# Gated delta rule: decay matrices from rows of running sums instead of a matrix product, and another table of stages

## The chip, the cores and the metric

The kernel runs on one core of one Trainium2 chip. The metric is the device time of one execution in microseconds (us), as the median of three runs. Engines: PE multiplies matrices, DVE and ACT work elementwise, POOL (GpSimd) does slower elementwise work, SP only issues DMAs.

## What is computed

Two decoder layers over 2048 tokens of width 1024: a gated delta rule (8 heads of 128), then an attention layer with forget gates. The change lies in the first. Cut to what matters:

```
gcum  = cumsum(g)                                   # g: log decay, per token and head
diff  = gcum[..., :, None] - gcum[..., None, :]
decay = where(causal, exp(diff), 0)
a_mat = where(strict, (beta k) k^T * decay, 0)
sol   = triangular_solve(I + a_mat, [beta v, beta k exp(gcum)])
attn  = q k^T * decay
# then, chunk by chunk: v_new = u - w S;  o = q exp(g) S + attn v_new;  S = S exp(g_last) + k_dec^T v_new
```

In the kernel a chunk has 128 tokens, and `decay` of one head is a tile E of 128x128 for each of the four chunks of a quarter.

## The kernel before, in words

The delta-rule phase takes the first 1185 us or so. It runs over four quarters of 512 tokens, and in each over four pairs of heads. `project` (L272) makes one pair: for each head the tiles k, q, v (in this order, kinds 1, 0, 2; tile number `ct` = kind x 8 + head), then two z tiles. A tile is eight k-steps of three 128x512 matmuls (`mm3`, L129 to L132: float32 split in a high and a low part), collected in a PSUM buffer `pp`, which ACT and DVE empty a little later (`cx`, `acc`, `th`, `kq`; transposes `pt`). In quarter 0 the weights are loaded as they are (`wr`), cast on ACT (`wh`), the rest taken on POOL (`wl`, L296), and both kept in DRAM (`w_d`) for the other quarters.

Ahead of a head's first tile L325 to L332 make its E: POOL multiplies an upper triangle with g, as a high and a low part (`rg`, two instructions), PE multiplies both with a strict lower triangle (`pdf`, L329, two matmuls), which gives all the differences of running sums, ACT takes the exp from PSUM (L331), POOL sets what lies above the diagonal to zero (L332).

`finish` (L418) inverts the unit triangular matrices of a pair and runs the recurrence. Diagonal blocks of 32x32 go to DRAM and back in another layout (`d1`, `Ai`), DVE eliminates (`tmp`, `Ti`), the blocks return (`d2`, `At`), DVE transposes three of four (`Tn`, L447). Small products on PE then join blocks to 64 (`px` L453, copied to `X` by ACT L457 and DVE L458; `py` L464) and to 128 (`px` with 64x64, `py` with 64x64). After that comes the recurrence (`pa`, `o`, `R`, `w`, `S`), then the norm and the gate (`og`).

`weave` (L589) runs the two together: at every k-step of the current pair's `project` the previous pair's `finish` may take a step; a `yield n` in `finish` lets n further k-steps pass. The stage lengths stand in one line (L583): `W_INV` k-steps between the start of the inverse and `px`, `W_PY` from `px` to `py`, and so on. A scheduler of the framework sets the final order of each engine when the kernel is built, going by the order of the program; each engine then runs its own list in order and waits for semaphores. An SP, ACT or POOL instruction that waits therefore holds up all that stands behind it on its engine.

## Time and profile before

| | |
|---|---|
| three runs | 2913.45, 2918.45, 2922.11 us; median 2918.45 |
| the profiled execution | 2933.14 us, its span 2931.4 us |
| mean granted clock of PE | 0.982 of full speed |
| PE busy | 2814.7 us, 96% |
| DVE, ACT, POOL busy | 1718.0 (59%), 1334.9 (46%), 707.4 (24%) us |
| moved by DMA | 371.64 MB |

Durations below come from the profiled execution. In a timeline row the first number is the start in us, the second the busy time of the row's instructions, `x2` their count, and the bracket the idle time of the engine before it and what ended that. Buffer numbers are left out of names, so `pp_q` is any projection tile of that kind.

### The profile page before, as it was taken

Reading aid. Unit: us, or ns where it says so; the run is one execution under the profiler, and the core shown is the slowest. Engines: PE = TensorE matmul, PEld = TensorE weight load, DVE = VectorE, ACT = ScalarE, POOL = GpSimd, SP = SyncE. Lnnn points to the kernel's source line nnn. Section 1 sums busy time; section 2 is a strip of 40 time slices with the busy share of each in tenths; the row PEclk is TensorE's granted clock in tenths of the full one; section 3 lists DMA queues with packets and bytes.
Section 4 is the critical chain, followed back from the end, with each engine's and each line's share of the span. In section 5 each row is a group of like instructions: output and inputs, shape, how many; then the busy total and the mean of one; then the engine's idle time right before and its main releaser. Section 6 shows DMA issues by size and latency. Waiting matters only on the chain. (4 is left out here: it accounts for less than half of the span.)

```text
span 2931.4 us, 50710 instructions
## 1 busy us (share of the span) xinstructions
PE 2814.7 (96%) x18406; PEld 2446.1 (83%) x18406; DVE 1718.0 (59%) x5053; ACT 1334.9 (46%) x3695; POOL 707.4 (24%) x713
## 2 busy tenths in 40 slices
PE   7898999999999999989999999999999999999998
PEld 5677788878887878778999999999997888888787
DVE  5767876777777776644333124332228888888422
ACT  4445544454445444434344223443326777776421
POOL 5544211111111111123211000110004444443322
PEclk9999999999999999989999999999999999999999
DMA  6565544444453443645322233332322332332443
GB/s 222 177 185 187 170 135 138 151 148 150 136 160 120 150 147 107 193 127 181 94 87 87 92 97 112 97 97 93 102 76 87 101 97 91 98 93 81 151 144 108
DMA packets 295505, 371.64 MB, mean 127 GB/s; under 512 B 68443, under 2 KB 216150, under 8 KB 294230
## 3 DMA queue, kind: packets, MB, share of 16 engines
q1 hardware_dynamic: 295254, 368.39, 39.6%
q8 instruction: 145, 2.38, 0.3%
q14 instruction: 106, 0.87, 0.1%
HBM read 263.40 MB, written 104.92 MB: 126 GB/s over the span
## 5 line engine op out<-in xcount | busy, mean ns | idle before, releaser
L130 PE MATMUL pp_q<-xh_q,wh_q 128*128 128x512 f32 x768 | 327.4, 426 | 3.4 <-ACT wh_q L294 1.9
L132 PE MATMUL pp_q<-xh_q,wl_q 128*128 128x512 f32 x768 | 308.8, 402 | 0.0
L131 PE MATMUL pp_q<-xl_q,wh_q 128*128 128x512 f32 x768 | 307.5, 400 | 0.0
L351 DVE SCALAR_TENSOR_TENSOR acc_q<-cx_q,cols,acc_q 128x512 f32<-128x512 f32 x288 | 225.9, 784 | 13.3 <-ACT acc_q L349 10.0
L125 DVE TENSOR_TENSOR pl<-pt,ph 128x512 fp32r<-128x512 f32 (+1 forms) x320 | 191.8, 605 | 39.5 <-ACT ph L124 37.6
L124 ACT CAST ph<-pt 128x512 fp32r<-128x512 f32 (+1 forms) x320 | 161.6, 519 | 92.8 <-PE pt L1077 91.9
L354 ACT ACTIVATE th_q<-acc_q 128x512 f32<-128x512 f32 x96 | 60.6, 632 | 285.7 <-DVE acc_q L351 282.3
L1063 ACT ACTIVATE s<-s,nm 128x128 f32<-128x128 f32 (+15 forms) x128 | 154.2, 1205 | 73.6 <-DVE nm L1061 73.4
L1077 PE MATMUL pt<-ident,s 128*128 128x128 f32 x1088 | 173.8, 274 | 2.7 <-DVE pl L125 2.4
L132 PEld LDWEIGHTS pp_q<-xh_q,wl_q 128*128 128x128 f32 x768 | 146.7, 191 | 34.9 <-POOL wl_q L296 0.4
L130 PEld LDWEIGHTS pp_q<-xh_q,wh_q 128*128 128x128 f32 x768 | 146.9, 191 | 29.8 <-ACT wh_q L294 2.0
L131 PEld LDWEIGHTS pp_q<-xl_q,wh_q 128*128 128x128 f32 x768 | 147.4, 192 | 26.3
L1077 PEld LDWEIGHTS pt<-ident,s 128*128 128x128 f32 x1088 | 134.5, 141 | 33.3 <-DVE pl L125 3.5
L130 PE MATMUL ppk<-wh_k,hh 128*128 128x256 f32 x512 | 148.2, 289 | 2.6 <-issue 2.6
L130 PE MATMUL ppq<-wh_q,hh 128*128 128x256 f32 x512 | 146.8, 287 | 0.0
L131 PE MATMUL ppk<-wl_k,hh 128*128 128x256 f32 x512 | 145.0, 283 | 0.0
L130 PE MATMUL ppv<-wh_v,hh 128*128 128x256 f32 (+1 forms) x512 | 144.9, 283 | 0.0
L132 PE MATMUL ppk<-wh_k,hl 128*128 128x256 f32 x512 | 144.8, 283 | 0.0
L130 PE MATMUL ppz<-wh_z,hh 128*128 128x256 f32 x512 | 144.3, 282 | 0.0
L132 PE MATMUL ppv<-wh_v,hl 128*128 128x256 f32 (+1 forms) x512 | 144.0, 281 | 0.0
L131 PE MATMUL ppv<-wl_v,hh 128*128 128x256 f32 (+1 forms) x512 | 143.9, 281 | 0.0
L132 PE MATMUL ppq<-wh_q,hl 128*128 128x256 f32 x512 | 143.7, 281 | 0.0
(479 smaller groups left out, 8592.7 us busy)
## 6 DMA issues: line engine op xcount, KB each, us to landing
wh_q<-w_d SPq DMA_DIRECT2D x72, 512.0 KB, 3.7
wl_q<-w_d SPq DMA_DIRECT2D x72, 512.0 KB, 5.0
wr_q<-in_gdn_w_in_dram SPq DMA_DIRECT2D x24, 512.0 KB, 6.4
w_d<-wh_q SPq DMA_DIRECT2D x24, 512.0 KB, 4.7
w_d<-wl_q SPq DMA_DIRECT2D x24, 512.0 KB, 3.5
wh_q_z<-w_d SPq DMA_DIRECT2D x24, 512.0 KB, 3.5
wl_q_z<-w_d SPq DMA_DIRECT2D x24, 512.0 KB, 4.4
x_q<-in_x_dram SPq DMA_DIRECT2D x16, 512.0 KB, 4.2
```

The costliest lines, as they stand in the source:

```text
L124: i = k.nc.scalar.copy(hi, src)
L125: (eng or k.nc.vector).tensor_tensor(out=lo, in0=src, in1=f(hi), op=ALU.subtract)
L130: nc.tensor.matmul(out, ah, bh, start=start, stop=False)
L131: nc.tensor.matmul(out, ah, bl, start=False, stop=False)
L132: nc.tensor.matmul(out, al, bh, start=False, stop=stop)
L351: nc.vector.scalar_tensor_tensor(out=acc, in0=cx[:, j:j + TB], scalar=cw[j], in1=acc, op0=ALU.mult, op1=ALU.add)
L354: nc.scalar.activation(th, acc, AF.Tanh, scale=0.5)
L1063: e = nc.scalar.activation(s[:, 0:w], s[:, 0:w], AF.Exp, bias=nm, accum_out=ls[:, ii:ii + 1])
L1077: nc.tensor.transpose(out=pt[:, ii * P:(ii + 1) * P], in_=Ps[ii][:, j * P:(j + 1) * P], identity=k.ident)
```

## The change

The preparation of a quarter no longer splits g. It transposes the running sums `gc` (a PE transpose, 128x32 to 32x128), copies them to SBUF (`gT`) and keeps another copy (`gs`) beside. `decays`, called after a head's q tile, replaces the product: for the first head of a quarter it writes `gT` to DRAM (`g_d`) and loads that head's row, spread over all partitions, into `gb`, both on POOL's DMA queue; for every head but the last it issues the load of the next head's row on SP's queue (256 KB in SBUF). POOL then subtracts the column `gs` from the row, sets what lies above the diagonal to a large negative number, and ACT takes the exp from SBUF into E. In the table, `W_INV` goes from 45 to 43, `W_PY` from 5 to 6, `W_PY2` from 2 to 3; the total is the same.

```diff
-        gh = p2.tile([P, CH, H], F32R, tag="gh", name=f"gh_{q_}")
-        nc.vector.tensor_copy(gh, g)
-        gl = p2.tile([P, CH, H], F32R, tag="gl", name=f"gl_{q_}")
-        nc.vector.tensor_tensor(out=gl, in0=g, in1=f(gh), op=ALU.subtract)
...
+        pgT = pq.tile([CH * H, P], F32, tag="kkq", name=f"pgT_{q_}")
+        nc.tensor.transpose(out=pgT, in_=gcf[:, 0, :], identity=k.ident)
+        gT = p1.tile([CH * H, P], F32, tag="gT", name=f"gT_{q_}")
+        nc.vector.tensor_copy(gT, pgT)
+        g_d = pd.tile([CH, H, P], F32, tag="g_d", name=f"g_d_{q_}")
+        gs = p2.tile([P, CH, H], F32, tag="gs", name=f"gs_{q_}")
+        nc.vector.tensor_copy(gs, gc[:, 0])
...
+        def rows(h, dma):
+            gb = gbs[h] = p2.tile([P, CH, P], F32, tag="gb", name=f"gb_{q_}_{h}")
+            dma.dma_start(gb, g_d[:, h].unsqueeze(0).to_broadcast([P, CH, P]))
+
+        def decays(h, E):
+
+            if h == 0:
+                nc.gpsimd.dma_start(g_d.rearrange("c h t -> (c h) t"), gT)
+                rows(0, nc.gpsimd)
+            if h < H - 1:
+                rows(h + 1, nc.sync)
+            gb = gbs.pop(h)
+            nc.gpsimd.tensor_tensor(out=gb, in0=gb, in1=gs[:, :, h:h + 1].to_broadcast([P, CH, P]), op=ALU.subtract)
+            nc.gpsimd.affine_select(out=gb, in_=gb, pattern=[[0, CH], [1, P]], compare_op=ALU.is_ge,
+                                    fill=NEG, base=0, channel_multiplier=-1)
+            nc.scalar.activation(E, gb, AF.Exp)
...
-            rg = p1.tile([P, 2, CH, P], F32R, tag="rg", name=f"rg_{q_}_{h}")
-            for i, gg in enumerate((gh, gl)):
-                nc.gpsimd.tensor_tensor(out=rg[:, i], in0=bc(k.tri, CH),
-                                        in1=f(gg[:, :, h:h + 1]).to_broadcast([P, CH, P]), op=ALU.mult)
-            pdf = pq.tile([P, CH, P], F32, tag="kkq", name=f"pdf_{q_}_{h}")
-            for i in range(2):
-                nc.tensor.matmul(pdf.rearrange("p a b -> p (a b)"), k.lowr,
-                                 rg[:, i].rearrange("p a b -> p (a b)"), start=i == 0, stop=i == 1)
-            nc.scalar.activation(E, pdf, AF.Exp)
-            nc.gpsimd.affine_select(out=E, in_=E, pattern=[[0, CH], [1, P]], compare_op=ALU.is_ge,
-                                    fill=0.0, base=0, channel_multiplier=-1)
...
+                if kind == 0:
+                    decays(h, E)
...
-W_INV, W_PY, W_PX2, W_PY2, W_A, W_B, W_C, W_OUT, W_OUT2 = 45, 5, 4, 2, 2, 1, 2, 9, 1
+W_INV, W_PY, W_PX2, W_PY2, W_A, W_B, W_C, W_OUT, W_OUT2 = 43, 6, 4, 3, 2, 1, 2, 9, 1
```

How the built order of the engines differs, at two places. The first is the inverse of the first head pair of quarter 1 (`q1g`), while the v tile of head 3 (`pp_q_19`) is projected. A row is line, operation, output and inputs with buffer numbers, size, and what it waits for (`DMAHW`: a transfer). On PE, before:

```order
L130 MATMUL pp_q_19_4810<-xh_q_6_3318,wh_q_19_4806 128x512
L131 MATMUL pp_q_19_4810<-xl_q_6_3326,wh_q_19_4806 128x512
L132 MATMUL pp_q_19_4810<-xh_q_6_3318,wl_q_19_4807 128x512
L366 MATMUL pt_q_11_4844<-ident,kq_q_3_4632 128x128 [waits DVE_49]
L366 MATMUL pt_q_11_4844<-ident,kq_q_3_4632 128x128 x3
L453 MATMUL px_q1g_4861<-Tn,At_q1g_3454 32x32 [waits DVE_49,PE_49]
L453 MATMUL px_q1g_4861<-Tn,At_q1g_3454 32x32 [waits DVE_49]
L453 MATMUL px_q1g_4861<-Tn,At_q1g_3454 32x32 x14
L130 MATMUL pp_q_19_4810<-xh_q_7_3319,wh_q_19_4806 128x512
```

On PE there, after:

```order
L124 MATMUL pp_q_19_4804<-xh_q_4_3308,wh_q_19_4800 128x512
L125 MATMUL pp_q_19_4804<-xl_q_4_3316,wh_q_19_4800 128x512
L126 MATMUL pp_q_19_4804<-xh_q_4_3308,wl_q_19_4801 128x512
L460 MATMUL px_q1g_4832<-Tn,At_q1g_3449 32x32 [waits DVE_49,PE_49]
L460 MATMUL px_q1g_4832<-Tn,At_q1g_3449 32x32 [waits DVE_49]
L460 MATMUL px_q1g_4832<-Tn,At_q1g_3449 32x32 x14
L124 MATMUL pp_q_19_4804<-xh_q_5_3309,wh_q_19_4800 128x512
```

`px` has moved from behind k-step 6 and the transposes `pt` to behind k-step 4.

On DVE at the same place, before:

```order
L359 SCALAR_TENSOR_TENSOR kq_q_3_4632<-th_q_11_4741,acc_q_11_4736 128x4x128 [waits Activation_49]
L558 SCALAR_TENSOR_TENSOR og_q_6_4788<-pto_q_6_4779,hon,zT_q0g_2425 128x512 [waits PE_49]
L447 STREAM_TRANSPOSE Tn<-At_q1g_3454 32x8x32 [waits DMAHW0_49]
L447 STREAM_TRANSPOSE Tn<-At_q1g_3454 32x8x32 [waits DMAHW1_49]
L346 COPY halo<-cx_q_3_4794 128x3 [waits Activation_49]
L447 STREAM_TRANSPOSE Tn<-At_q1g_3454 32x8x32 [waits DMAHW2_49]
L351 SCALAR_TENSOR_TENSOR acc_q_3_4798<-cx_q_3_4794,cols,acc_q_3_4798 128x512 [waits Activation_49]
```

On DVE there, after:

```order
L565 SCALAR_TENSOR_TENSOR og_q_6_4775<-pto_q_6_4766,hon,zT_q0g_2421 128x512 [waits PE_49]
L366 SCALAR_TENSOR_TENSOR kq_q_3_4627<-th_q_11_4728,acc_q_11_4723 128x4x128 [waits Activation_49]
L454 STREAM_TRANSPOSE Tn<-At_q1g_3449 32x8x32 [waits DMAHW4_49]
L353 COPY halo<-cx_q_3_4788 128x3 [waits Activation_49]
L358 SCALAR_TENSOR_TENSOR acc_q_3_4792<-cx_q_3_4788,cols,acc_q_3_4792 128x512 [waits Activation_49]
L454 STREAM_TRANSPOSE Tn<-At_q1g_3449 32x8x32 [waits DMAHW5_49]
L454 STREAM_TRANSPOSE Tn<-At_q1g_3449 32x8x32 [waits DMAHW6_49]
```

The first `acc` of tile 3 has moved ahead of the second and third `Tn`, and `og` ahead of `kq`.

On ACT at the same place, before:

```order
L349 ACTIVATE acc_q_3_4798<-pp_q_3_4748,cols 128x512
L354 ACTIVATE th_q_3_4803<-acc_q_3_4798 128x512 [waits DVE_49]
L370 ACTIVATE j_q_11_0_4849,ssn_q_3_4644<-pt_q_11_4844 128x128 [waits PE_49,Activation_49,Pool_49]
L370 ACTIVATE j_q_11_1_4851,ssn_q_3_4644<-pt_q_11_4844 128x128 [waits Activation_49]
L370 ACTIVATE j_q_11_2_4853,ssn_q_3_4644<-pt_q_11_4844 128x128 [waits Activation_49]
L370 ACTIVATE j_q_11_3_4855,ssn_q_3_4644<-pt_q_11_4844 128x128 [waits Activation_49]
L373 ACTIVATE kd_q_3_4634<-pt_q_11_4844,eg_q_3450 128x128 x4
L457 COPY X_q1g_4878<-px_q1g_4861 32x256 [waits PE_49]
```

On ACT there, after:

```order
L326 ACTIVATE E_q_4_5066<-gb_q_4_4781 128x512 [waits DVE_49,Pool_49]
L361 ACTIVATE th_q_11_4728<-acc_q_11_4723 128x512 [waits DVE_49]
L407 ACTIVATE vR_q_2_4261<-pt_q_18_4757,vs_q_2_4266 128x128 [waits PE_49]
L407 ACTIVATE vR_q_2_4261<-pt_q_18_4757,vs_q_2_4266 128x128 x3
L352 COPY cx_q_3_4788<-pp_q_3_4735 128x512 [waits PE_49]
L356 ACTIVATE acc_q_3_4792<-pp_q_3_4735,cols 128x512
L464 COPY X_q1g_4849<-px_q1g_4832 32x256 [waits PE_49]
L361 ACTIVATE th_q_3_4797<-acc_q_3_4792 128x512 [waits DVE_49]
```

The copy `X` has moved from behind `th`, `j` and `kd` to straight behind `acc`; the exp of a later head's E stands some rows ahead.

The second place is POOL at the first heads of quarter 0, before:

```order
L325 TENSOR_TENSOR rg_q_0_344<-tri,gh_q_321 128x512 [waits DVE_49]
L325 TENSOR_TENSOR rg_q_0_344<-tri,gl_q_323 128x512 [waits DVE_49]
L296 TENSOR_TENSOR wl_q_16_448<-wr_q_16_449,wh_q_16_447 128x256 [waits DMAHW0_49,Activation_49]
L296 TENSOR_TENSOR wl_q_16_448<-wr_q_16_449,wh_q_16_447 128x256 x3
L325 TENSOR_TENSOR rg_q_1_516<-tri,gh_q_321 128x512 [waits PE_49]
L332 AFFINE_SELECT E_q_0_343<-E_q_0_343 128x512 [waits Activation_49]
```

On POOL there, after:

```order
L318 DMA g_d_q_327<-gT_q_325 32x128 [waits DVE_49]
L295 TENSOR_TENSOR wl_q_16_449<-wr_q_16_450,wh_q_16_448 128x256
L313 DMA gb_q_0_427<-g_d_q_327 128x4x128 [waits DMASW0_49]
L295 TENSOR_TENSOR wl_q_9_521<-wr_q_9_522,wh_q_9_520 128x256 [waits DMAHW3_49,Activation_49]
L295 TENSOR_TENSOR wl_q_9_521<-wr_q_9_522,wh_q_9_520 128x256 x3
L323 TENSOR_TENSOR gb_q_0_427<-gb_q_0_427,gs_q_328 128x512 [waits DMASW1_49]
L323 TENSOR_TENSOR gb_q_1_429<-gb_q_1_429,gs_q_328 128x512 [waits DMAHW5_49]
L324 AFFINE_SELECT gb_q_0_427<-gb_q_0_427 128x512 [waits Pool_49]
```

E of head 0 now hangs on two transfers one after the other and on what stands between them on POOL; the exp of that E stands on ACT ahead of `cx` and `acc` of tile 0.

## Rows read from the trace of the kernel before

**Rows 1.** The page, part 1: busy us, share and instructions of each engine.

```profile
PE 2814.7 (96%) x18406; PEld 2446.1 (83%) x18406; DVE 1718.0 (59%) x5053; ACT 1334.9 (46%) x3695; POOL 707.4 (24%) x713
```

**Rows 2.** Waits of PE, 0 to 1260 us: releaser, us in total, times, longest.

```profile
PE py_q1g L464 <- ACT X_q1g L457: 3.3, 4, 1.1
...
PE pdf_q L329 <- POOL rg_q L325: 2.0, 5, 0.7
...
PE py_q2g L464 <- ACT X_q2g L457: 1.9, 2, 0.9
...
PE py_q1g L464 <- DVE X_q1g L458: 0.9, 4, 0.2
```

**Rows 3.** Timeline of PE, 475 to 477 us, one decay product.

```profile
475.84 0.71 PE L329 MATMUL pdf_q<-rg_q,lowr 128*128 128x512 f32 x2
476.38 0.40 PE L130 MATMUL pp_q<-xh_q,wh_q 128*128 128x512 f32 x1
...
477.09 0.39 PE L130 MATMUL pp_q<-xh_q,wh_q 128*128 128x512 f32 x1
```

**Rows 4.** Timeline of PE, 452 to 460 us, `px` and `py` of `q1g`.

```profile
452.70 0.24 PE L453 MATMUL px_q1g<-Tn,At_q1g 32*32 32x32 f32 x2
453.35 0.69 PE L453 MATMUL px_q1g<-Tn,At_q1g 32*32 32x32 f32 x30 [0.40 <-DVE Tn L447]
...
459.35 0.24 PE L464 MATMUL py_q1g<-At_q1g,X_q1g 32*32 32x32 f32 x2 [0.93 <-ACT X_q1g L457]
```

**Rows 5.** Timeline of DVE, 450 to 455 us.

```profile
450.46 0.69 DVE L359 SCALAR_TENSOR_TENSOR kq_q<-th_q,acc_q 128x512 f32<-128x512 f32 x1 [0.49 <-ACT th_q L354]
...
451.74 0.89 DVE L447 STREAM_TRANSPOSE Tn<-At_q1g 32x256 f32<-32x256 f32 x2
...
452.86 0.43 DVE L447 STREAM_TRANSPOSE Tn<-At_q1g 32x256 f32<-32x256 f32 x1
453.32 1.54 DVE L351 SCALAR_TENSOR_TENSOR acc_q<-cx_q,cols,acc_q 128x512 f32<-128x512 f32 x2
```

**Rows 6.** Timeline of ACT, 451 to 459 us.

```profile
451.80 0.73 ACT L349 ACTIVATE acc_q<-pp_q,cols 128x512 f32<-128x512 f32 x1
...
458.94 0.36 ACT L457 COPY X_q1g<-px_q1g 32x256 f32<-32x256 f32 x1
```

**Rows 7.** Timeline of PE at 590 us, `px` in the v tile of head 7.

```profile
590.70 0.69 PE L453 MATMUL px_q1g<-Tn,At_q1g 32*32 32x32 f32 x32
```

**Rows 8.** Timeline of DVE there.

```profile
589.41 0.44 DVE L447 STREAM_TRANSPOSE Tn<-At_q1g 32x256 f32<-32x256 f32 x1
```

**Rows 9.** Timeline of ACT at 48 us, tile 0 of quarter 0.

```profile
48.44 0.70 ACT L349 ACTIVATE acc_q<-pp_q,cols 128x512 f32<-128x512 f32 x1
```

**Rows 10.** Timeline of PE at 54 us, the first matmul of tile 9.

```profile
54.29 0.39 PE L130 MATMUL pp_q<-xh_q,wh_q 128*128 128x512 f32 x1
```

**Rows 11.** Timeline of PE at 201 and at 304 us, two waits.

```profile
201.21 0.66 PE L366 MATMUL pt_q<-ident,kq_q 128*128 128x128 f32 x4 [1.72 <-DVE kq_q L359]
...
304.32 0.85 PE L453 MATMUL px_q0g<-Tn,At_q0g 32*32 32x32 f32 x30 [2.25 <-DVE Tn L447]
```

**Rows 12.** The page, part 6: DMA issues, KB each, median us to landing.

```profile
wl_q<-w_d SPq DMA_DIRECT2D x72, 512.0 KB, 5.0
```

**Rows 13.** The tile `d_q1g`: issue to landing of its transfers.

```profile
DMA to landing us min/median/max: 1.5/2.0/3.9
```

**Rows 14.** Stretches: length, busy and (count) of PE, PEld, DVE, ACT, POOL, PE clock, DMA share, GB/s.

```profile
201.00:208.00 7.00, 6.79 (x40) 5.90 (x41) 7.00 (x15) 2.81 (x13) 4.54 (x5) 1.00 0.72 206
226.20:233.00 6.80, 4.49 (x40) 3.64 (x41) 4.98 (x11) 4.59 (x17) 4.08 (x4) 0.50 0.46 178
304.70:308.10 3.40, 3.40 (x25) 2.76 (x20) 1.78 (x4) 2.99 (x14) 0.00 (x0) 0.50 0.43 128
461.70:465.10 3.40, 3.40 (x11) 2.75 (x10) 2.91 (x7) 1.66 (x9) 0.26 (x1) 0.50 0.04 10
```

**Rows 15.** Timeline of POOL, 438 to 447 us.

```profile
443.38 1.64 POOL L119 TENSOR_TENSOR rn_q<-ssn_q,mhalf 128x8 f32<-128x8 f32 x1 [2.13 <-DVE ssn_q L376]
```

More of the change, by code (lines that the diff above doesn't have):

```diff
@@ L58, in setup @@
     sb0 = sp.enter_context(k.tc.tile_pool(name="sb0", bufs=1, side="left"))
-    low = sb0.tile([P, P], F32, name="low")
-    nc.gpsimd.affine_select(out=low, in_=k.ones, pattern=[[-1, P]], compare_op=ALU.is_gt,
-                            fill=0.0, base=0, channel_multiplier=1)
-    k.lowr = cp.tile([P, P], F32R, name="lowr")
-    nc.vector.tensor_copy(k.lowr, low)
     k.mhalf = cp.tile([P, 8], F32, name="mhalf")
@@ L191, in gdn @@
     kept = []
+    gbs = {}
     def keep():
@@ L268, in prep @@
         nc.vector.tensor_scalar(out=neg, in0=eg[:, 0], scalar1=-1.0, scalar2=None, op0=ALU.mult)
-        return xh, xl, beta, gh, gl, eg, neg
+        return xh, xl, beta, gs, (gT, g_d), eg, neg
     def project(qt, hg, state, tiles):
-        xh, xl, beta, gh, gl, eg, neg = state
+        xh, xl, beta, gs, (gT, g_d), eg, neg = state
         q_ = f"q{qt}"
```

## The prediction

> **What bounds the kernel now.** I read the busy line of the page first: PE is busy 2814.7 us of a 2931.4 us span [rows 1]. Where PE is that full, a saving counts only if it takes an instruction out of PE's stream or shortens a stretch in which PE stands still. So next came PE's list of waits for the part that the change touches [rows 2], and then PE, DVE and ACT row by row around one inverse, that of the first head pair of quarter 1, at 450 to 460 us [rows 4 to 6]. The reader is to see there a race that is lost by a hair: PE comes to the small products `px`, starts the first two at 452.70, and finds the last transposed tile `Tn` 0.40 us late [rows 4]. Of the twelve head pairs of quarters 1 to 3, six look like that (`px` lies in the v tile of head 3 or head 5; I call them A). Three have `px` in the v tile of head 7 (C): there the last `Tn` ended 0.85 us before `px` began, 589.41 + 0.44 against 590.70 [rows 7, 8]. The last three (D) fall into the next quarter and have more room still.
>
> **What goes: the decay products.** Each of 32 heads loses two 128x512 matmuls `pdf` on PE. The pair starts at 475.84 and the next projection matmul at 476.38, and three projection matmuls behind it take 477.09 - 476.38 = 0.71, that is 0.237 each [rows 3]. So a pair is worth 0.47 (two such steps) to 0.54 (start to start); I take the first, since it is the pitch of everything around it: 32 x 0.466 = **-14.9 us**, and -17.3 at the other end. All of it lies on PE, hence on the path. PE also waited 2.0 us, five times, for POOL's factor `rg` [rows 2]; nobody on PE waits for the new `gb` directly: **-2.0**. The POOL products, the exp on ACT and the mask on POOL are replaced one for one or fall away on engines that PE does not wait for there; they count as nothing, and the cover is gone only where a head's E comes late (below).
>
> **What is added on PE.** Four transposes of the running sums, one a quarter, at about a projection step each (0.24) [rows 3]: **+1.0**. The other additions of the preparation (two small copies on DVE) stand between `gc` and the exp of `eg`, and PE has projection steps to do there.
>
> **What is moved: the W table.** The total of steps is the same; the first stage is two steps shorter, the second and the fourth one longer. As the order shows, `px` stands two k-steps (six matmuls) and four transposes earlier in the v tile: 6 x 0.237 + about 0.5 = 1.9 us less of PE's time in front of it. PE therefore stands at `px` at 452.70 - 1.9 = 450.8. What does DVE do meanwhile? In before it runs without a break from 450.46: `kq`, `og`, two `Tn`, the third `Tn` at 452.86 to 453.3, then the first `acc` of the next tile at 453.32 [rows 5]. In after the `og` comes ahead of `kq` and fills the 0.49 that DVE idled for ACT, so the first `Tn` ends some 0.5 earlier than 452.2, at 451.75; but the second and third stand behind the `acc` of tile 3, and that needs ACT's `acc`, which ends at 451.80 + 0.73 = 452.53 [rows 6]. A DVE `acc` takes 0.77 (1.54 for two) and a `Tn` 0.44 [rows 5]: 452.53 + 0.77 + 0.88 = 454.2. So PE waits 1.0 at the first product and then until 454.2, 3.2 in all against 0.40: +2.8, six times: **+16.8**. For C the order puts one `Tn` behind one `acc`: 589.41 + 0.77 + 0.44 = 590.6 against PE's arrival at 590.70 - 1.9 = 588.8, **+1.7 each, 5.1**. In D there is room: 0.
>
> The other end of these waits. Ahead of that stretch DVE stands for POOL's `rn`, 1.64 us long, and POOL loses one of its three operations of a head. If DVE got that time back, the waits of A would shrink to about 1.6 and those of C to nearly nothing; but POOL had itself been idle for 2.13 us until DVE's `ssn` came, so there is no queue to shorten [rows 15]. If ACT's `acc` is held up by the exp of E, which in after stands a few rows ahead of it, they grow by at most its length, about that of an `acc`, 0.73. I take the plain reading of the rows.
>
> **What it pays back: `py`.** In before the copy of `X` on ACT stood behind eight small activations and began at 458.94, 5 us after `px` was done, and PE waited 0.93 for it at 459.35 [rows 4, 6]. In after the copy stands straight behind `px` on ACT, and `py` has one step more. So these waits go: 3.3 + 1.9 + 1.9 on ACT's half (quarter 3's line reads like quarter 2's) and 2.5 on DVE's (three lines of 0.9, 0.9 and 0.7, the first of them in the rows) [rows 2]: **-9.6**. To bring them back ACT would have to be some 5 us late.
>
> **Quarter 0's first head.** Its row is the one load that nothing precedes: g to DRAM and back on POOL's queue. No POOL-queue transfer is in the trace; the nearest landings are loads of 512 KB on SP's queue at 5.0 us, and the small ones of the inverse at 2.0 us [rows 12, 13]. Two of 2 to 5 us from about 38 us on give 43 to 48; POOL then has four weight pieces, the subtraction and the mask to do, so E's exp would end at 51 to 53, and behind it on ACT stand `cx` and `acc` of tile 0, whose `acc` ran at 48.44 in before; PE needs that PSUM buffer at 54.29, less the two `pdf` pairs ahead of it now gone, 53.4 [rows 9, 10]. The wait is 0 to 5; I take **+2**. SP's queue holds the second head's row ahead of two weight transfers and its third head's row, which waits for the exp of the first E, ahead of a weight load; what that delays is read and split well ahead of its use, and I leave it inside those 0 to 5. In quarters 1 to 3 the first product with E comes a k, a q and half a v tile after the sums are there, so the same chain is covered. The rows themselves (32 loads of 256 KB) go by DMA engines that PE does not wait for: nothing.
>
> The Trainium skill speaks against the POOL-queue DMAs: "SBUF — State Buffer", section "SBUF: two separate sides", says that descriptors of a DMA issued on GpSimd wait while VectorE runs a two-port operation, and gives about 620 ns alone against 3100 ns beside one. No run here shows it. By that figure the two first loads would be some 5 us later in all, an estimate, and the sum 5 us higher; the sum here goes by the bounds above.
>
> **The clock.** A wait of 1.72 us at 201.21 was followed by the full granted clock (1.00, that is 2.4 GHz, from 201 to 208), one of 2.25 at 304.32 by 3.4 us at half of it (0.50, 1.2 GHz), and the waits around 226 us by 6.8 us of half clock [rows 11, 14]. At half clock 3.4 us do the work of 1.7. The waits that I expect in A come as 1.0 and 2.2, between the first two rows: I charge half of 6 x 1.7: **+5.1** (0 to 10.2). The half clock after two of the `py` waits (461.7 to 465.1 is one of the two [rows 14]) goes: **-3.4**.
>
> **The sum:** -14.9 - 2.0 + 1.0 + 16.8 + 5.1 - 9.6 + 2.0 + 5.1 - 3.4 = **+0.1 us**. The profiled execution took 2933.14 us against a median of 2918.45; the sum is a difference within that one execution, and I carry it to the median: 2918.5. Ends of the terms give -18 to +20 around it.
>
> **Rivals.** (1) *The `px` waits don't grow.* DVE comes to `Tn` two to three us earlier against PE, because it has to run a backlog off there (from 450.46 to 454.8 it has no gap) that began some tiles before, where its order has changed too: E comes from SBUF early, and nothing waits for a mask. For it: with `py` without waits each pair's inverse goes on sooner; against it: the `acc` that stands between the `Tn` and hangs on ACT, and a POOL without a queue [rows 5, 15]. It leaves out 16.8, 5.1 and 5.1: -27 + 0.1, **2892**, faster. (2) *The clock falls at every `px`.* The place is the v tile of nine head pairs; the point from which it decides is a wait of about 2.25 us, where rows show half clock. Price: two windows (6.8 us, 3.4 lost) after each of six, one after each of three: 20.4 + 5.1 instead of 5.1, that is +20: **2939**, slower. For it: 1.0 + 2.2 is above the mark as a whole; against it: a product runs between the pieces. (3) *The table does not do what it says*, the first stage is short enough already and the order hardly alters `px`: the order shows otherwise, so no chance of its own.
>
> **How the numbers follow.** The forecast has a chance of 0.48, its own range 2903 to 2932; rival 1 has 0.25, rival 2 0.27. A measurement of this kernel can tell about 0.3% from no change, that is 2909.7 to 2927.2. The forecast puts 0.13 below that, 0.28 within and 0.07 above; rival 1 0.25 below; rival 2 0.02 within and 0.25 above. So faster 0.38, same 0.30, slower 0.32. The range that leaves out two in ten reaches to both rivals: 2890 to 2941.
>
> **What would show it.** The `pdf` rows gone and POOL's `rg` with them; the `px` rows of A with about 3 us of waiting, of C with 1.7, `py` with none; PE's busy time less by about 15 us before clock; the first `acc` of tile 0 near 52 us. The forecast is wrong if the `px` waits stay under 1 us (rival 1), or if the granted clock reads 0.5 after each of them (rival 2); also if a projection waits for weights whose loads stand behind a row load on SP.

## The result and the profile after

The changed kernel takes 2949.65 us against 2918.77 us of the kernel before on the same chip: ratio 1.0102, 95% interval 1.0088 to 1.0116, about 30 us slower. The forecast was no change (2918.5), the range ended at 2941. 2949.65 is the median of four executions, of which one took 3354.11 us at a mean granted clock of 0.761; without that one, which the ratio leaves out, it is 2949.1. The profiled execution of after took 2946.1 us, its span 2944.3.

The page of after, part 1 (busy us, share, instructions), answers to [rows 1]:

```profile
PE 2803.7 (95%) x18346; PEld 2442.4 (83%) x18346; DVE 1698.6 (58%) x5052; ACT 1336.2 (45%) x3695; POOL 678.6 (23%) x688
```

PE has 60 instructions less (64 `pdf` gone, 4 transposes new), and is busy 11 us less than in [rows 1]. So the product is gone, and yet the kernel is slower: the time went into standing still and into clock. PE's waits, 28 to 1290 us (releaser, us in total, times, longest), answer to [rows 2]:

```profile
PE px_q0g L460 <- DVE Tn L454: 15.2, 5, 4.9
PE pt_q L373 <- DVE kq_q L366: 13.1, 6, 5.1
PE pp_q L124 <- ACT acc_q L356: 6.5, 4, 2.6
PE px_q2g L460 <- DVE Tn L454: 6.0, 3, 2.3
PE px_q1g L460 <- DVE Tn L454: 6.0, 3, 2.3
PE px_q3g L460 <- DVE Tn L454: 6.0, 3, 2.3
PE pa_q0g L506 <- DVE vR_q L541: 5.8, 4, 2.7
PE pp_q L124 <- DVE zT_q0g L421: 5.5, 1, 5.5
```

The waits at `rg` have left the list, and those at `py` are down to 0.6 us in all, as forecast. In their place stand nine waits at `px` (three a quarter in quarters 1 to 3, 6.0 us each quarter) and waits of the projection and of `pa`, of which only one, 2.56 us for the first `acc`, was forecast. PE, then DVE and ACT at the first pair of quarter 1, timelines, answer to [rows 4, 5]:

```profile
460.70 0.24 PE L460 MATMUL px_q1g<-Tn,At_q1g 32*32 32x32 f32 x2
463.20 0.69 PE L460 MATMUL px_q1g<-Tn,At_q1g 32*32 32x32 f32 x30 [2.26 <-DVE Tn L454]
464.88 0.63 PE L124 MATMUL pp_q<-xh_q,wh_q 128*128 128x512 f32 x1
465.31 0.63 PE L125 MATMUL pp_q<-xl_q,wh_q 128*128 128x512 f32 x1
```

```profile
460.04 0.43 DVE L454 STREAM_TRANSPOSE Tn<-At_q1g 32x256 f32<-32x256 f32 x1
461.47 0.75 DVE L358 SCALAR_TENSOR_TENSOR acc_q<-cx_q,cols,acc_q 128x512 f32<-128x512 f32 x1 [0.42 <-ACT acc_q L356]
462.25 0.90 DVE L454 STREAM_TRANSPOSE Tn<-At_q1g 32x256 f32<-32x256 f32 x2
```

```profile
460.70 0.73 ACT L356 ACTIVATE acc_q<-pp_q,cols 128x512 f32<-128x512 f32 x1
```

This is the mechanism of the forecast: the second and third `Tn` stand behind an `acc` that waits for ACT (the last row, of ACT, answers to [rows 6]). But look at the matmuls behind it: they start 0.43 apart instead of 0.237. The clock has fallen. Stretches (length, busy and count of PE, PEld, DVE, ACT, POOL, then PE's granted clock, DMA share, GB/s):

```profile
457.40:460.80 3.40, 3.40 (x19) 2.56 (x17) 3.00 (x6) 2.09 (x7) 0.00 (x0) 1.00 0.12 43
464.30:467.70 3.40, 3.40 (x12) 2.70 (x11) 2.29 (x5) 0.99 (x4) 0.00 (x0) 0.50 0.46 128
467.70:471.10 3.40, 3.40 (x29) 2.51 (x31) 0.66 (x2) 2.88 (x13) 0.00 (x0) 1.00 0.91 53
600.80:604.20 3.40, 3.40 (x36) 2.71 (x33) 3.15 (x6) 0.99 (x2) 0.00 (x0) 0.51 0.90 321
365.30:372.10 6.80, 4.69 (x18) 4.20 (x19) 6.16 (x21) 3.01 (x10) 2.39 (x2) 0.50 0.53 162
```

Full clock (1.00, 2.4 GHz) before the wait at 460.94, 3.4 us at half (0.50, 1.2 GHz) behind it, then full again. The fourth row is a pair C, where the wait was 1.46 us; the fifth the first head of quarter 1. Of the nine pairs A and C, eight have such a stretch; a wait of 2.24 us at 1039 has none.

What a whole pair costs is seen in stretches from one pair's first `px` to the next's. Before (a second profiled execution, 2922.12 us, span 2920.4), then after:

```profile
518.60:586.70 68.10, 66.52 (x437) 54.98 (x437) 49.04 (x172) 30.74 (x105) 8.65 (x7) 1.00 0.47 151
667.30:735.00 67.70, 66.36 (x437) 54.92 (x436) 48.93 (x168) 31.25 (x107) 10.65 (x9) 1.00 0.44 137
```

```profile
460.80:529.80 69.00, 66.74 (x433) 55.28 (x433) 47.02 (x168) 30.89 (x107) 8.79 (x7) 0.98 0.51 151
685.20:750.20 65.00, 65.00 (x434) 54.05 (x434) 47.13 (x167) 30.79 (x107) 8.98 (x7) 1.00 0.51 159
```

The last row is a pair without wait: PE busy from end to end, 65.0 us. The same pair of before is the row at 667.30. That is what the rows are worth: 2.7 us there, half of it work (66.36 to 65.0) and half idle time. The row above it, at 460.80, is a pair with a `px` wait: 69.00 - 66.74 = 2.26 of idle time, and about the *same* work now takes 66.74 instead of 65.0, 1.7 more, which is half of 3.4 us. Together 4.0, and the pair is slower than before (68.1).

Added up over the trace of both, in us (I sum PE's idle time, count half of PE's busy time at half clock as lost, and call the remainder work; the second execution of before is the base):

| stretch | before | after | work | idle | half clock |
|---|---|---|---|---|---|
| to `px` of the 4th pair | 382.7 | 391.2 | -9.0 | +12.6 | +4.9 |
| nine intervals inside quarters | 611.2 | 614.7 | -13.9 | +4.1 | +13.2 |
| three intervals over a quarter's turn | 248.7 | 262.5 | -3.7 | +7.0 | +10.3 |
| the rest of the program | 1677.8 | 1675.9 | -0.2 | +1.2 | -2.8 |
| span | 2920.4 | 2944.3 | -27.0 | +25.0 | +25.9 |

The split is rough: kernels with more waits show less work, so idle time and clock are charged somewhat too high and work too low by as much. The sums are exact: everything is lost before the 16th pair, nothing in the attention layer.

One execution can be a chance, but span and mean granted clock are on record for every run, and span x (1 - clock) is what the clock took. It took 37.5 us on average in the 64 executions of before that ran beside the experiments, and 73.7 in the other three of after; what is left of the span is 2880.8 and 2873.0. At full clock after would thus be some 8 us faster than before; the clock costs it 36 us more. Up to 6 of these are half clock during waits, where it costs nothing (24.3 us at half clock against 12.8 in the two profiled executions, at half weight).

### The profile page after: what moved, and what is told of

Read it like the earlier page. It is cut to its first block, busy times and chain, and to the rows that moved or that the text cites. A ratio compares the mean times of both kernels' runs of the same rounds, so it can differ in the third digit from the quotient of the medians.

```text
span 2944.3 us, 50701 instructions
## 1 busy us (share of the span) xinstructions
PE 2803.7 (95%) x18346; PEld 2442.4 (83%) x18346; DVE 1698.6 (58%) x5052; ACT 1336.2 (45%) x3695; POOL 678.6 (23%) x688
## 4 chain that ended last, share of the span: by engine, by line
PE 64%; DVE 15%; issue 5%; ACT 3%; DMA 3%; POOL 2%; SPq 0%; DVEq 0%; POOLq 0%; ACTq 0%
DVE acc_q L358 4%; PE pt L1084 4%; PE ps L126 2%; PE ppv L124 2%; PE ppq L124 2%; PE pp_q_z L124 2%; PE ppv L125 2%; PE ppv L126 2%; PE ppq L125 2%; PE ppq L126 2%; PE ppwf L126 2%; PE ppwf L125 2%; PE ppwf L124 2%; PE ppk L124 2%; PE ps L124 2%
## 5 line engine op out<-in xcount | busy, mean ns | idle before, releaser
L124 PE MATMUL pp_q<-xh_q,wh_q 128*128 128x512 f32 x768 | 336.9, 439 | 13.8 <-ACT acc_q L356 6.5
L125 PE MATMUL pp_q<-xl_q,wh_q 128*128 128x512 f32 x768 | 314.1, 409 | 0.0
L124 PEld LDWEIGHTS pp_q<-xh_q,wh_q 128*128 128x128 f32 x768 | 150.5, 196 | 41.3 <-ACT acc_q L356 8.2
L125 PE MATMUL ppq<-wl_q,hh 128*128 128x256 f32 x512 | 143.7, 281 | 0.0
```

The lines of the kernel that those rows point to most:

```text
L124: nc.tensor.matmul(out, ah, bh, start=start, stop=False)
L125: nc.tensor.matmul(out, ah, bl, start=False, stop=False)
```

## The experiments

Theories as the expectations name them: A, two prices, that of the table (`px` waits and clock) and that of the first heads; B, the table alone; C, the row transfers as such; D, the exp of E waits for a free E buffer; E, ACT loses because it stands in order at that exp. (The pairs A, C and D of the prediction have nothing to do with these letters.) Each ratio is to the kernel before on the same chip. A "due step" in the expectations is a k-step.

### Table and rows apart

`e1_rows_old_table` is after with `45, 5, 4, 2` in the table; `e2_product_new_table` is before with the new one:

```diff
-W_INV, W_PY, W_PX2, W_PY2, ... = 45, 5, 4, 2, ...
+W_INV, W_PY, W_PX2, W_PY2, ... = 43, 6, 4, 3, ...
```

> The changed kernel with the table of before (45, 5, 4, 2): rows from DRAM alone. Theory A (the added 31 us are two prices, the table's waits at px with half clock behind them, and the first head of each quarter that waits for its row; the product's 15 us on PE are saved): the table's price goes, the first heads' stays, and the waits at py of 0.9 us come back: 2920 to 2935 us, with waits of PE at px below 1.6 us in quarters 1 to 3 and the waits of the first projection after E at 364 us unchanged (about 1.4 and 2.7 us). Theory B (the table alone): 2900 to 2908. Theory C (the rows alone, by their transfers): 2945 to 2955.

> The kernel before with the new table (43, 6, 4, 3): the stages alone. Theory A: the waits at px of about 2.3 us in the v tiles of heads 3 and 5 and about 1.5 us in that of head 7, each followed by 3.4 us of half clock, and no waits at py: 2928 to 2940 us. Theory B (the table alone): 2955 to 2965 us, since the product's matmuls are still there. Theory C (the rows alone): 2913 to 2923 us.

Measured: e1 2935.35 us, 1.0064 (1.0039 to 1.0089); e2 2935.27, 1.0056 (1.0037 to 1.0075). Each half costs about 16 us, and the two add up. Theories B and C fall by both runs as the whole cause, and so does the thought that either half was good; theory A has e2 and misses e1 by 0.35 us. In e2 there is no row load at all; `px` waits there 1.36 + 0.83:

```profile
454.85 0.21 PE L453 MATMUL px_q1g<-Tn,At_q1g 32*32 32x32 f32 x2 [1.36 <-DVE Tn L447]
455.89 0.69 PE L453 MATMUL px_q1g<-Tn,At_q1g 32*32 32x32 f32 x30 [0.83 <-DVE Tn L447]
```

In the nine intervals inside quarters e2 has 14.3 us of idle time against 12.3 before: what `px` costs, `py` had cost before, so in idle time the table is nearly free. But its half-clock stretches there come to 34 us, against none, and the nine take 625.9 against 611.2. That execution is the slowest of e2's seven (2943.0 us). Over all seven the clock took 50.3 us against 37.5 in before, and 2883.0 is left against 2880.8: the table's price is clock. The rows alone (e1) leave 2872.0, 9 less than before, and the clock takes 60.9.

A second look at before itself belongs here:

> The kernel before, unchanged, for a second profile on this chip: its first profiled execution took 2933 us and its timed ones 2913 to 2922. All theories: 2912 to 2935 us; which stretches differ between its two profiles shows how much of a stretch's difference to the changed kernel is the kernel.

It took 2922.12 us, where the first profiled execution had taken 2933.14. The half clock at 461.7 [rows 14] isn't there in the second one, nor behind any other `py` wait of 0.93 inside quarters 1 to 3. The same code at the same places had half clock in one execution and not in the other.

### The first head of a quarter

`e6_first_head_product` is after with the product for head 0 of each quarter, and rows for heads 1 to 7 (`gT` to DRAM on SP):

```diff
+            if h == 0:
...
+                    nc.tensor.matmul(pdf.rearrange("p a b -> p (a b)"), k.lowr,
+                                     rg[i].rearrange("p a b -> p (a b)"), start=i == 0, stop=i == 1)
+                nc.scalar.activation(E, pdf, AF.Exp)
```

> The changed kernel, but the first head of each quarter takes its E from the matrix product as before, so no E waits for the trip to DRAM and back; the running sums are written to DRAM on SP's queue, the other seven heads load rows as in the change. Eight matmuls of 0.23 us come back. Theory A: PE's waits of 2.6 us at 54 us, and of 1.4 and 2.7 us at 364 and 1.9 and 2.6 at 660 us go with the half clock behind them: 2925 to 2937 us. Theory B (the table alone) and C by the transfers as such: 2945 to 2953 us, since 28 of 32 rows are still loaded and the table is the new one.

Measured: 2940.3 us, 1.0083 (1.0061 to 1.0106): 9 less than after by the medians, but the intervals of the two ratios overlap, and it lies between the forecasts of A and of C. The fourth pair's `px` starts 5.7 us sooner, at 385.5 against 391.2; the three turns take 264.6, no less than the 262.4 of after. (The run e9 below measures this price better.) How the price comes about is seen in after at the turn to quarter 1, POOL, ACT, DVE and PE:

```profile
357.69 1.43 POOL L323 TENSOR_TENSOR gb_q<-gb_q,gs_q 128x512 f32<-128x512 f32 x1 [2.52 <-DMA gb_q<-g_d_q]
360.40 1.05 POOL L323 TENSOR_TENSOR gb_q<-gb_q,gs_q 128x512 f32<-128x512 f32 x1 [1.28 <-DMA gb_q<-g_d_q]
361.41 1.23 POOL L324 TENSOR_SCALAR_AFFINE_SELECT gb_q<-gb_q 128x512 f32<-128x512 f32 x2
```

```profile
362.67 0.63 ACT L326 ACTIVATE E_q<-gb_q 128x512 f32<-128x512 f32 x1 [4.79 <-POOL gb_q L324]
363.21 0.67 ACT L356 ACTIVATE acc_q<-pp_q,cols 128x512 f32<-128x512 f32 x1
```

```profile
363.91 0.75 DVE L358 SCALAR_TENSOR_TENSOR acc_q<-cx_q,cols,acc_q 128x512 f32<-128x512 f32 x1 [3.72 <-ACT acc_q L356]
```

```profile
363.93 0.50 PE L124 MATMUL pp_q<-xh_q,wh_q 128*128 128x512 f32 x1 [1.41 <-ACT acc_q L356]
367.41 0.80 PE L506 MATMUL pa_q0g<-S,kq_q 128*128 128x128 f32 x2 [2.75 <-DVE vR_q L541]
```

The mask of head 0 stands on POOL behind a subtraction that waits for *head 1's* row; ACT waits 4.79 us at the exp, with the `acc` of a projection behind it; PE waits for that, and DVE too (3.72), so that `vR` behind DVE's `acc` is late and PE waits for it as well; PE runs 6.8 us at half clock (the row at 365.30 above). The turn was called covered in the prediction.

`e5_sp_loads` moves the first head's two transfers from POOL's queue to SP's:

```diff
-                nc.gpsimd.dma_start(g_d.rearrange("c h t -> (c h) t"), gT)
-                rows(0, nc.gpsimd)
+                nc.sync.dma_start(g_d.rearrange("c h t -> (c h) t"), gT)
+                rows(0, nc.sync)
```

> The changed kernel, but the first head's two transfers go on SP's queue instead of POOL's. If the POOL queue itself makes them late, PE's waits of 2.6 us at 54, of 1.4 and 2.7 at 364 and of 1.9 and 2.6 at 660 us go and the time falls by 8 us or more, to about 2940; if it is the trip to DRAM and back and the order of POOL's instructions, whichever queue, it stays within 5 us of 2950.

Measured: 2952.93, 1.0111 (1.0081 to 1.0142): no gain. Yet the waits themselves went or shrank: the 2.56 us at 54 are gone, and at the turn to quarter 1 there is no wait for `acc` any more and one of 1.14 us for `vR` instead of 2.75, without half clock. The three turns take 257.8 instead of 262.4, but the first quarter 400.8 instead of 391.2, with half clock from 156.0 to 179.9. So this run does not clear POOL's queue of a part in the first heads' waits; what it wins there the first quarter loses, and why is not isolated. DMA issues of after (KB each, median us to landing):

```profile
gb_q<-g_d_q SPq DMA_DIRECT2D x28, 256.0 KB, 6.5
gb_q<-g_d_q POOLq DMA_DIRECT2D x4, 256.0 KB, 8.6
```

The Trainium skill's warning ("SBUF — State Buffer", section "SBUF: two separate sides") that was weighed in the prediction would, as an estimate from its two figures, make two loads on the POOL queue some 5 us later in all. The 2.1 us between the medians of the two queues may be part of that, but no run separates it from the other differences of those four loads.

### The exp of E in ACT's order

In after ACT waits about 111 us in all at the exp of E (28 to 1290 us); in the kernel before 3.7, all of it for `pdf`. Waits of ACT in after, the lines of E:

```profile
ACT E_q L326 <- POOL gb_q L324: 24.5, 4, 7.8
ACT E_q L326 <- DVE halo L353: 24.3, 4, 7.3
ACT E_q L326 <- DVE attn_q1g L403: 17.8, 6, 5.4
ACT E_q L326 <- DVE attn_q0g L403: 15.9, 3, 6.7
ACT E_q L326 <- DVE attn_q2g L403: 14.4, 5, 4.9
ACT E_q L326 <- DVE attn_q3g L403: 13.8, 5, 4.9
```

The exp's only inputs are the row and a free E buffer (two, the older one is read last by `attn`), and the scheduler put it early. The longest wait of PE in that time, 5.49 us in quarter 0, lies beside one of these. ACT, then PE, DVE and POOL of after, and last the same row of DVE in before (second execution):

```profile
96.92 0.63 ACT L326 ACTIVATE E_q<-gb_q 128x512 f32<-128x512 f32 x1 [6.72 <-DVE attn_q0g L403]
```

```profile
97.47 0.80 PE L124 MATMUL pp_q<-xh_q,wh_q 128*128 128x512 f32 x1 [5.49 <-DVE zT_q0g L421]
```

```profile
92.88 0.68 DVE L385 TENSOR_SCALAR rq_q0g<-rn_q 128x4 f32<-128x4 f32 x1 [3.34 <-POOL rn_q L113]
96.74 0.68 DVE L421 SCALAR_TENSOR_TENSOR zT_q0g<-thz_q,pp_q_z 128x512 f32<-128x512 f32 x1
```

```profile
89.48 1.04 POOL L323 TENSOR_TENSOR gb_q<-gb_q,gs_q 128x512 f32<-128x512 f32 x1
90.59 0.64 POOL L324 TENSOR_SCALAR_AFFINE_SELECT gb_q<-gb_q 128x512 f32<-128x512 f32 x1
91.20 1.64 POOL L113 TENSOR_TENSOR rn_q<-ssn_q,mhalf 128x8 f32<-128x8 f32 x1
```

```profile
87.99 0.69 DVE L378 TENSOR_SCALAR rq_q0g<-rn_q 128x4 f32<-128x4 f32 x1 [1.76 <-POOL rn_q L119]
```

The exp does not stop PE here: it ends at 97.55, when PE already runs, and the `zT` that releases PE had stood behind DVE's wait for POOL's `rn`. POOL has the row's subtraction and mask in front of `rn`, which in before came straight behind weight pieces; DVE therefore waits 3.34 us instead of 1.76, and PE with it. The runs below agree. In e10 the exp is held elsewhere and PE still waits 5.16 us at that place; in e13 and e15 subtraction and mask run ahead of the weight pieces, DVE waits 1.79 and 1.78 us for `rn`, and PE 2.98 and 2.38.

Three kernels give E a third buffer: with the new table, with the old one, and with the old one and the product for head 0.

```diff
-            E = p2.tile([P, CH, P], F32, tag="E", name=f"E_{q_}_{h}")
+            E = p2.tile([P, CH, P], F32, tag="E", bufs=3, name=f"E_{q_}_{h}")
```

> The changed kernel, with three buffers for E instead of two, so that the exp of a head needn't wait until E of two heads before has been read by DVE (ACT stood 86 us behind these exps in the changed kernel, in quarters 1 to 3 about 5 us each, against 4 us in the kernel before, where the product's place in PE's order kept the exp behind). Theory D (the rows cost what ACT loses while its exp waits for a free E): 2932 to 2942 us, and ACT's waits at the exp for DVE's attn under 10 us; what is left over the kernel before is the table's 16 us and the first heads, less the product. Theory C (the transfers as such): 2945 to 2953. Theory A of the first submission (first heads and table only): 2944 to 2952.

> Rows from DRAM, the table of before, three buffers for E. Theory D: the table's 16 us and the waits for E are both gone, the first heads are left: 2912 to 2926 us. Theory C: 2930 to 2938, as with two buffers.

> As the run before, and the first head of each quarter takes its E from the product. Theory D: nothing of the three prices is left and 56 matmuls of 0.23 us are saved: 2902 to 2914 us, faster than the kernel before. Theory C: 2926 to 2934.

Measured: e7 2955.98, 1.012 (1.0096 to 1.0144); e8 2935.17, 1.0047 (1.0029 to 1.0065); e9 2921.67, 1.0002 (0.9988 to 1.0017). D falls: in e7 the exp is set still earlier and waits for the row instead (46.5 us, 9 times, for POOL's `gb`), and e8 comes out where C had it. But e9 is level with before, the first kernel with rows that is, though ACT still waits 91.5 us there at the exps of rows. It differs from e8 by the product for head 0 alone: that is worth 13.5 us with the old table, and the two intervals lie apart. Its pairs are of two kinds:

```profile
458.10:527.20 69.10, 66.91 (x434) 55.62 (x434) 48.16 (x170) 30.85 (x105) 6.60 (x5) 0.98 0.46 144
527.20:592.30 65.10, 65.10 (x434) 54.38 (x434) 46.92 (x169) 29.48 (x103) 4.91 (x3) 1.00 0.47 151
```

In the first kind the exp stands in front of the copy of `X` (64x64 step), and `py` waits 1.79 us with half clock behind it, ACT and PE:

```profile
474.30 0.63 ACT L337 ACTIVATE E_q<-gb_q 128x512 f32<-128x512 f32 x1 [4.63 <-DVE attn_q1g L426]
474.95 0.58 ACT L509 COPY X_q1g<-px_q1g 64x512 f32<-64x512 f32 x1
```

```profile
475.58 1.14 PE L514 MATMUL py_q1g<-At_q1g,X_q1g 64*64 64x64 f32 x16 [1.79 <-ACT X_q1g L509]
```

Next, the exp was tied to a tile of its own head by a bias column that is zero times that tile, so that the scheduler can't set it earlier. First to the q tile (column made on DVE), with the new table, the old one, and `46, 6, 4, 2`:

```diff
-            nc.scalar.activation(E, gb, AF.Exp)
...
+                    if kind == 0:
+                        nc.vector.tensor_scalar(out=zb, in0=src[:, 0, 0:1], scalar1=0.0, scalar2=None, op0=ALU.mult)
+                        nc.scalar.activation(E, gb, AF.Exp, bias=zb)
```

> The kernel after, with the exp of E written behind the q tile of its head and tied to it by a bias column of zeros made from the normalised q, so that ACT cannot come to it before the row has long landed and the E buffer of two heads before is free. Theory E (ACT loses in order: it stands at an exp that was placed before its row or its buffer was ready, about 111 us in all at line 326 in the kernel after, and late copies behind it hold TensorE): the waits of ACT at E fall to under 20 us, the four first heads' gaps shrink, and the time falls by 12 to 30 us, to 2918 to 2938; the table's own 16 us (the product kernel with the new table) remains. Theory C (the 26 loads of 256 KB as such cost the time, by their queue or their traffic): 2943 or more.

> The same with the table of before (45, 5, 4, 2). Theory E: the product's 13 to 15 us are saved and nothing is put in their place, so 2902 to 2922, faster than before. Theory C: 2928 or more, near the 2935 of the rows with the old table.

> The same with 46, 6, 4, 2, which sets px in the pairs A one due step later and the inverse's py after the z tile. If the waits at px and py are what is left, this one has under 1 us at each of px and py in the pairs A, fewer half-clock windows, and 5 to 12 us less than the held exp with the old table. If only the exp mattered, the two agree within 4 us.

Measured: e10 2955.82, 1.0118 (1.0093 to 1.0142); e11 2937.55, 1.0053 (1.0032 to 1.0074); e12 2991.47, 1.0235 (1.0214 to 1.0256). ACT's waits at E fell from 111 us to 16.9, 16.4 and 13.4, and the time did not follow: theory E falls as the cause of the loss (e10 and e11 come out where C had them). In e11 the exp's place on ACT changed the order of DVE: `px` now waits 1.8 us in the pairs A (only two of the six have half clock behind it) and `py` 1.4 in seven pairs. In e12 the `px` of 64x64 waits 2.2 to 3.7 from 400 us on, and the transposes `pto` 26.4 us in all (320 to 1290 us). "Later" is no cure by itself.

Then the exp was tied to the k tile instead (column made on POOL; two E buffers again), with the product or a row for head 0, and with both tables. With rows for all heads the loads are issued a tile earlier too, and head 0's exp stays behind its q tile:

> Rows for heads 1 to 7 of each quarter, the product for head 0, the table of before (45, 5, 4, 2), and the exp of E written behind the k tile of its own head, tied to that tile by a bias column of zeros which POOL makes. In the program the second X copy of a pair then stands on ACT directly behind the z tile's tanh, with no exp in front. Theory E (a pair costs what TensorE works, 65.1 us, plus its waits, plus half of its half-clock time; the waits at the second py come from an exp in front of the X copy): the six pairs A go from 69.1 to 69.7 us with three E buffers to 65 to 66, so 2895 to 2910, faster than before. Rival (the loads themselves cost, or other copies take the exp's place): A pairs of 68 us or more and 2918 or more.

> The same with the table 43, 6, 4, 3. Theory E: px waits of 1.4 to 2.3 us come back in nine pairs, with a half-clock stretch of 3.4 us behind most of them, 3 to 4 us each, so 25 to 35 us over the same kernel with the old table. Rival: with ACT free the copy of acc goes ahead and px no longer waits; then the two agree within 6 us.

> Rows for all heads, old table, held exp behind the k tile, except that head 0 of a quarter has its loads issued at its k tile and its exp behind the q tile. Theory E: the pairs as in the kernel with the product for head 0; the four first heads cost 0 to 4 us each, so 0 to 15 us above that kernel, 2897 to 2922. Rival (loads cost as such): 2930 or more, as the rows with the old table.

> As the one before, with the table 43, 6, 4, 3. Theory E: 25 to 35 us above the one before, and at most 2945; of the kernel after it differs by the held exp alone, which gains 5 to 25 us. Rival: within 6 us of the kernel after.

Measured: e13 2927.06, 1.0021 (1.0009 to 1.0032); e14 2947.59, 1.0095 (1.0079 to 1.0111); e15 2929.95, 1.0039 (1.0027 to 1.0052); e16 2959.78, 1.0136 (1.012 to 1.0153). I had expected 2895 to 2910 of e13, at most 2922 of e15, and of e16 a gain over after; it is 10 us slower. The `py` wait did go, but the third `Tn` now stands behind an `acc` that waits for ACT, and `px` waits 2.3 us again. A pair of e13 (the same pair takes 71.5 us in e16, and 65.0 where there is neither wait nor half clock):

```profile
453.60:523.60 70.00, 67.66 (x433) 56.40 (x434) 48.75 (x169) 30.83 (x106) 9.20 (x9) 0.95 0.50 149
```

Two half-clock stretches lie in it (clock 0.95), and PE's busy time is 67.7. The new table costs 20.5 (e14 over e13) and 29.8 us (e16 over e15) here, and between 14 and 21 in the other four couples that differ by it alone. Between e15 and e13, head 0 by row or by product, lie 3 us, less than the two intervals tell apart: with its loads issued a tile earlier the first head's price is nearly gone. Theory C, loads that cost as such, has its numbers met by e8, e10 and e11, but little other support: e9 with 28 of the 32 loads is level with before, and pairs with loads and without waits take 65.0 us.

### The second `py` alone

Last, e9 with the second `py` two or three k-steps later (`45, 5, 4, 4` and `45, 5, 4, 5`):

> Rows for heads 1 to 7, the product for head 0, three E buffers, and the table 45, 5, 4, 4: of the kernel with 45, 5, 4, 2 it differs by the second py alone, which stands two due steps (six projection matmuls, 1.4 us) later, where the X copy that it waited for 1.5 to 2.2 us is nearly done. If a pair's time is 65.1 us plus its waits plus half of its half-clock time, the pairs A fall from 69.1 to 69.7 to 66 to 67 and the time by 10 to 22 us, to 2900 to 2912, faster than before. Rival: the scheduler's order of DVE at Tn changes with it and px waits in place of py; then 2916 or more.

> The same with 45, 5, 4, 5: the second py three due steps later. By the same law no wait at py is left, 2896 to 2910. Rival as above: in the program one more operation of acc stands before the second Tn here, so a px wait of 1 to 2 us in the pairs A and 2916 or more.

Measured: 2931.65, 1.0037 (1.0023 to 1.0051), and 2927.93, 1.0028 (1.0018 to 1.0037): slower than before and than e9, against what I expected. Inside quarters the law holds: with 5 no pair there has half clock, and the nine intervals take 601.4 us, the least of all kernels (before 611.2, after 614.7):

```profile
457.20:523.60 66.40, 65.60 (x432) 53.98 (x432) 47.99 (x168) 30.82 (x105) 6.66 (x5) 1.00 0.48 153
```

But the three turns take 256.6 instead of e9's 247.1, with 20.7 us of idle time and 17.2 at half clock (e9: 16.2 and 1.7); `pa` waits there for ACT's `o` (4.7 us once) and `pto` for DVE. And the first quarter (389.5) stays 7 us over before (382.7), in e9 as here, without any late first head. No kernel tried beats the kernel before; e9 equals it. By the runs' clocks about the products' worth is there: without what the clock took, e9 is left with 2869.6 us and e13 with 2868.0, against 2880.8 of before, 11 and 13 less. But the clock took 50.8 and 56.4 us from them, against 37.5.

## Why the prediction was wrong, point by point

In one sentence: the terms of the sum outside the clock were near (-1.6 forecast, -8 measured without what the clock took), and the clock term, forecast at +1.7, came to some +30 to +36 us; with it fell the two places where the prediction put the new order of the engines at nothing.

- **The products, -14.9, and `rg`, -2.0: right, somewhat small.** PE's work in a pair without waits fell by 1.4 (66.36 to 65.0; 66.5 to 65.1 in e9), for two heads, against 0.93 to 1.08 forecast. Over the whole program the remainder after idle time and clock is 14.6 us less in e17_py2_5 than in before; that kernel keeps four of the 32 products, so the forecast's figure for it, with the transposes, is 12.0.
- **`px`, +16.8 and +5.1: right in mechanism, too high in size.** 2.26 in the pairs A, 0.40 before: +1.9 instead of +2.8. PE came to `px` at 460.70, 0.73 us before ACT's `acc` ended; I had put it 1.73 before. C measured 1.46 against 1.7. Together 11 + 4 instead of 22.
- **`py`, -9.6: right.** All but 0.6 us of its waits are gone.
- **The clock, +5.1 - 3.4: the step that failed most.** I charged half a stretch after six waits, none after C, and took 3.4 us back for the stretches behind the old `py`. Measured: a stretch of 3.4 us or two behind five of six A and *all* C, though the wait of C is 1.46 us, below the 1.72 us that I had taken as harmless from one row [rows 11]. And the credit was none: it came from one execution of before, the second has no half clock there. Rows of one event can't tell a threshold, and a stretch at half clock must be seen in two executions before it counts as a cost that can be saved. Inside quarters and at the turns the clock comes to +23.5 instead of +1.7 (with the caution above on the split), over all runs and the whole program to +36. e2, where nothing but the table differs, shows it without the rows: +2.0 of idle time, 34 us more at half clock, +14.7 in the nine intervals of its profiled execution. That the waits bring the half clock is argued from their order in time; no run shows what decides it.
- **Quarter 0's first head, +2 (0 to 5): right at its place, but the stretch to the fourth pair's `px` lost 8.5 us.** PE waited 2.56 us at 53.79 for `acc`, which ran at 53.05, forecast "near 52", and 3.4 us at half clock followed. The row was forecast for 43 to 48 and POOL's subtraction began at 49.4 (its load, issued at 41.3, took 8 us, not 2 to 5); but the weight pieces that I had set behind it were done by then, and the exp began at 52.04, in the 51 to 53 of the forecast.
- **"Replaced one for one ... count as nothing": wrong.** Exp, subtraction and mask are as many as before, but they now wait for a load or a buffer, in order, in front of other work. Of PE's 5.49 us at 97.47 the 1.6 by which POOL's `rn` is later are theirs (in before PE stood 2.60 there, at `pdf`, a wait that the sum did not look at), and so are the turn's 1.41 + 2.75. I had seen the exp some rows ahead in ACT's order and asked only what it delays by its length (0.73), not what it waits for; and of POOL I had asked only what it no longer does, not what its two operations now stand in front of.
- **"In quarters 1 to 3 the same chain is covered": wrong.** See the rows at 357 to 367: some 4 us of waiting and 6.8 us at half clock at the turn to quarter 1, where before had waits of 1.3 and 0.6.
- **Rival 2 (2939) was the nearest:** the clock does fall at nearly every `px`. Its point of decision (2.25 us) was too high, its price for A (two stretches) too high too.

What stays open: whether a wait brings half clock. In e1 waits of 1.70 to 1.71 us at `py` are followed by it at 478 and 1044 us and not at 763; in e11 those of 1.8 at `px` are in two pairs of six; no rule from these runs settles it. Why the three turns cost 13.8 us with both changes, but 3.3 with the table alone and 2.8 with the rows alone. And what the remaining 7 us of quarter 0 are, in kernels with neither a late first head nor the new table: DVE's longer wait for POOL's `rn` is one part (15.5 us in e9 against 12.1 over the quarter); the order of DVE and ACT differs there throughout, and no run isolates one wait.

## What to carry to other kernels

When a matrix product on a full PE is replaced by a load, the instruction that consumes the load inherits its waits, and whatever a scheduler sets behind it on that engine waits too: list what stands behind it, and what each of its inputs, buffers included, waits for. But a long wait beside a stall is not its cause: follow the row that released PE back to the wait that ended last (here POOL's `rn`, not ACT's exp). On a PE that is never idle for long, price a new wait of 1.5 to 2.3 us at its length plus up to 1.7 for the clock, and look at the clock in two executions before crediting its return. A table of stages is tuned to one order of instructions: take a part of the program out, and the waits move from `px` to `py` and back, so change the table only with the trace of the new program in hand.

## What the hardware showed that I had not expected

- Half clock for 3.4 us after a wait of only 1.46 us (three times of three), and 6.8 from 658.9 on, behind a wait of 1.95 that ended at 658.4 and through one of 2.59; but none after waits of 1.8 in four pairs of e11, nor after the six `py` waits of 0.9 in the second execution of before.
- Two executions of the same kernel differ by 11 us of span (2931.4 and 2920.4), most of it half-clock stretches that one has and the other hasn't.
- A load of 256 KB that repeats one row on all partitions lands after 6.5 us (SP's queue) or 8.6 (POOL's), while 512 KB of weights took 5.0 [rows 12].
